# The second block's down product: tiles 0 and 1 as an eleventh pair in the second group, in place of two plain units

## The chip, the cores and the metric

The kernel runs on one core of a Trainium2 chip. The metric is the device time of one execution in microseconds (us); for each version the median of several runs is given. Engines are named as the profile names them: PE is TensorE's matmuls and PEld its weight loads, DVE is VectorE, ACT is ScalarE, POOL is GpSimd, SP is SyncE. SP and POOL do little here but issue DMA transfers; rows with SPq and POOLq are these issues.

## The reference, cut to what matters

One layer of a macaron block for 512 rows and a width of 1024, in fp32: a first feed-forward block, attention, and a second feed-forward block, which is the part that is changed. Behind it stands a last normalisation.

```python
def swiglu(x, w_gate, w_up, w_down):
    return (jax.nn.silu(x @ w_gate) * (x @ w_up)) @ w_down

x = x + 0.5 * swiglu(rmsnorm(x, ffn1_norm), ffn1_w_gate, ffn1_w_up, ffn1_w_down)
x = x + token_mixer(rmsnorm(x, mix_norm), w_in, w_out, ...)
x = x + 0.5 * swiglu(rmsnorm(x, ffn2_norm), ffn2_w_gate, ffn2_w_up, ffn2_w_down)
return rmsnorm(x, final_norm)
```

The inner width is 2816: 22 tiles of 128. Tile j of what `silu(...) * (...)` gives is called activation tile j here. In the code the first block has the name "a", the second the name "b", and buffers end in that letter.

## The kernel before

**Products in three parts.** An fp32 operand is split into a high and a low part, each of the type fp32r: ACT casts the high part, DVE subtracts it from the operand for the low one. A product is then three matmuls, high with high, high with low and low with high (`mm3`, L174 to L176), so every weight costs ACT one cast (L469) and DVE one subtraction (L473) before PE can read it.

**Seven products.** Gate, up and down are mostly computed by a scheme of Strassen's kind: a matrix product of 2 x 2 blocks by seven block products and some sums. A unit `("g", j)` or `("u", j)` gives the gate or up values of the two activation tiles j and j+1, in seven products of 12 matmuls of 256 columns; its banks are named pw, px, py, pz. The pair (j, j+1) is then kept for the down product by a chain of eleven steps (`kept`): four casts on ACT, and on DVE four low parts and three steps of sums and differences, the three largest of them of 512 columns. The results (h0, h1, h2, l0, l1, l2 and one more) go to the seven slots that `sets` names for the pair.

**The down product** adds 0.5 times `activations @ w_down` to x. It is done in two groups, `("t", 0)` for the pairs 2, 4, 6, 8, 10 and `("t", 1)` for the pairs 12, 14, 16, 18, 20. A group is seven products (a11, a22, s2, a12, s1, s3, s4 in the first, a11, s3, s2, a12, s1, a22, s4 in the second); a product takes each pair in turn, and for a pair it has two row tiles of three matmuls of 512 columns, into the banks pt. When a product ends, DVE adds its banks to x (L569), or ACT copies them into another bank. The weights are four blocks of 128x512 for each pair: a11 (buffer raa or rab, two pairs to a raw tile, of which there are three), a12 (rbb), a22 (reb) and the two sums s1 = a21 + a22 (sCb) and s3 = a11 + a21 (sBb). For a sum SP loads the first block (L523) and POOL adds the second with a transfer that accumulates (L524). s2 and s4 are made on DVE out of these blocks (L432).

**Tiles 0 and 1** of the activations do not belong to a pair in the second block. The front computes them as soon as the block begins (`gated`), splits them at once into ahb and alb (cast L927, subtraction L930), and two plain units multiply them: `("P", 0)` stands ahead of `("t", 0)` and gives the left half of the output columns, `("P", 1)` stands ahead of `("t", 1)` and gives the right half. Each has 24 matmuls of 512 columns into four banks pp, one raw tile of weights (rpb, two loads of 256 KB, split 1024 wide), and four additions to x. The first block has no plain units: there tiles 0 and 1 are multiplied in another way beside its second group.

**What sets the order.** All instructions are written out by one planner. `units` is the list of units in order; every product of one pair takes one STEP on the planner's clock (1410), and `starts` is their running sum. `at(time, rank, f)` puts an event on the planner's clock, and `run` writes them out in order of time and rank: the high part of a weight 4 STEP ahead of its product, the low part 3, a sum 5, a raw load 7, the weight sums 14. For the down groups, the table `ahead` gives for each block and pair how many STEP ahead of its group its load is issued; what isn't in it is loaded 8 STEP ahead of its product. `later` moves the split of single weights one STEP back. Each engine then runs its instructions in the order that they were written, and waits where data or a buffer isn't there. Split weights go through three places of two halves each (the buffer w in the trace), so a cast can wait for the matmuls that read what stood in that place before.

**The last product**, s4 of `("t", 1)`, is done tile by tile rather than pair by pair: its weights are all split before (`kept_weights`, kwb and kxb, at the times that TURNED_KEPT names) and its five pairs run first for one row tile and then for the other. Behind it stands the tail: squares on ACT (L2002), sums and factors on DVE (L2014 to L2016), scaling and the transfers to the output (L2025 to L2056).

## Time and profile before

| | before |
|---|---|
| runs, us | 914.67, 914.72, 916.83 (median 914.72) |
| profiled execution, us | 917.04 |
| its span, us | 915.2 |
| mean granted TensorE clock | 0.998 of full speed |
| instructions | 16047 |
| DMA | 143.88 MB, 157 GB/s mean |

The profile is of one execution; its span runs from the first to the last instruction that is recorded. A group of the profile is one line of the code, one engine and one operation, written with the buffers that it writes and reads (out<-in) and with the shape. Behind a number of instructions stand their busy time and the mean of one in ns, then the engine's idle time just before them and what ended it. A timeline row has the start in us, the duration in us, the engine and line, the operation and its buffers; in brackets stands how long the engine idled before it, and what released it. The matmuls are pipelined: the time from one start to the next is what a matmul costs, and the duration in its row is longer than that.

### The profile page before, as it was taken

What the parts mean: (1) busy time and instruction counts of PE and PEld (TensorE: products, weight loads), DVE (VectorE), ACT (ScalarE), POOL (GpSimd) and SP (SyncE); (2) the same over time, 40 slices, a digit from 0 to 9 for tenths busy, and PEclk for the clock granted to TensorE, in tenths of its full rate; (3) what the DMA queues carried; (4) which work ended last, traced back from release to release, by engine and by line L of the source; (5) the groups of instructions that cost most, each with busy time, mean ns of one, the idle gap of its engine ahead of it and who ended that gap; (6) DMA issues with size and microseconds to landing.
All of it is one profiled execution on the core that took longest, in us unless ns stands there. A gap on an engine that the chain in (4) does not pass through costs nothing.

```text
span 915.2 us, 16047 instructions
## 1 busy us (share of the span) xinstructions
PE 906.7 (99%) x5778; PEld 818.9 (89%) x5778; DVE 733.0 (80%) x1531; ACT 558.6 (61%) x1185; POOL 98.7 (11%) x123
## 2 busy tenths in 40 slices
PE   9999999999999999999999999999999999999997
PEld 7888998899998889888989778989999889999885
DVE  7698998878888886857865545898888887888886
ACT  6445765456567647656776675656666545666664
POOL 0000202121121100000000000011211212112200
PEclk9999999999999999999999999999999999999999
DMA  7354869677888613334433204365778869778822
GB/s 258 115 147 130 212 202 250 149 192 194 197 203 264 177 47 99 93 107 112 128 116 116 69 24 139 93 156 143 193 187 235 193 146 250 169 192 199 222 79 92
DMA packets 67247, 143.88 MB, mean 157 GB/s; under 512 B 7712, under 2 KB 8224, under 8 KB 67168
## 3 DMA queue, kind: packets, MB, share of 16 engines
q1 hardware_dynamic: 51312, 113.81, 38.7%
q0 software_dynamic: 15856, 29.06, 19.5%
q8 instruction: 45, 0.74, 0.3%
q14 instruction: 34, 0.28, 0.1%
HBM read 137.55 MB, written 2.14 MB: 153 GB/s over the span
## 4 chain that ended last, share of the span: by engine, by line
PE 96%; DVE 2%; ACT 1%; DMA 0%; issue 0%; DVEq 0%; SPq 0%; ACTq 0%
PE pt L176 6%; PE pt L175 6%; PE pt L174 6%; PE pq L174 2%; PE pwo L174 2%; PE pq L176 2%; PE pk L174 2%; PE pq L175 2%; PE pk L176 2%; PE pk L175 2%; PE pwo L176 2%; PE pwo L175 2%; PE pua L174 2%; PE pua L176 2%; PE pua L175 2%; PE pga L174 1%
## 5 line engine op out<-in xcount | busy, mean ns | idle before, releaser
L1736 ACT ACTIVATE pr<-pr,mx 128x128 f32<-128x128 f32 (+3 forms) x64 | 36.0, 563 | 36.7 <-DVE mx L1733 36.4
L569 DVE SCALAR_TENSOR_TENSOR x<-pt,x 128x512 f32<-128x512 f32 x52 | 34.5, 687 | 19.0 <-PE pt L176 11.7
L1733 DVE CUSTOM_DVE_ANT_0 pr<-sc,strip 128x128 f32<-128x128 f32 (+3 forms) x64 | 30.5, 489 | 23.1 <-PE sc L1731 22.6
L405 POOL DMA_DIRECT2D s1bg<-wst_dram x10 | 8.7, 866 | 331.8 <-DVE fin L1390 233.0
L473 DVE TENSOR_TENSOR w<-s2b,w 128x512 fp32r<-128x512 f32 x38 | 26.0, 685 | 7.2 <-ACT w L469 7.2
L469 ACT CAST w<-s2b 128x512 fp32r<-128x512 f32 x38 | 23.6, 620 | 7.3 <-DVE s2b L437 7.3
L469 ACT CAST w<-raa 128x512 fp32r<-128x512 f32 x31 | 18.9, 620 | 13.7 <-DVE raa L432 7.4
L174 PE MATMUL pwo<-w,mh 128*128 128x512 f32 x64 | 25.9, 405 | 0.0
L175 PE MATMUL pwo<-w,mh 128*128 128x512 f32 x64 | 25.0, 391 | 0.0
L176 PE MATMUL pwo<-w,ml 128*128 128x512 f32 x64 | 25.0, 391 | 0.0
L473 DVE TENSOR_TENSOR w<-s2a,w 128x512 fp32r<-128x512 f32 x30 | 20.6, 686 | 4.4 <-ACT w L469 4.3
L1524 DVE TENSOR_TENSOR w<-raw_qk,w 128x512 fp32r<-128x512 f32 x24 | 16.4, 687 | 7.9 <-ACT w L1520 7.8
L469 ACT CAST w<-s2a 128x512 fp32r<-128x512 f32 x30 | 18.6, 621 | 6.7 <-DVE s2a L437 6.2
L175 PE MATMUL pxgb<-ttb,w 128*128 128x256 f32 x80 | 22.5, 281 | 0.0
L469 ACT CAST w<-rab 128x512 fp32r<-128x512 f32 x26 | 15.9, 621 | 10.0 <-PE pt L176 5.6
L405 POOL DMA_DIRECT2D s1ag<-wst_dram x8 | 7.1, 887 | 130.7 <-DMA s1ag<-wst_dram 55.1
L473 DVE TENSOR_TENSOR w<-raa,w 128x512 fp32r<-128x512 f32 x31 | 20.7, 681 | 0.0
L1730 PE MATMUL sc<-k,q 128*128 128x128 f32 (+3 forms) x64 | 20.5, 322 | 0.0
L1731 PE MATMUL sc<-l,q 128*128 128x128 f32 (+3 forms) x64 | 20.2, 322 | 0.0
L175 PE MATMUL pxub<-ttb,w 128*128 128x256 f32 x72 | 20.2, 281 | 0.0
L175 PE MATMUL pwga<-xl,w 128*128 128x256 f32 x64 | 18.0, 281 | 0.0
L176 PE MATMUL pwga<-xh,w 128*128 128x256 f32 x64 | 18.0, 281 | 0.0
(1095 smaller groups left out, 3920.8 us busy)
## 6 DMA issues: line engine op xcount, KB each, us to landing
raw_qk<-wqk_dram SPq DMA_DIRECT2D x12, 512.0 KB, 3.6
raw0bg<-wst_dram SPq DMA_DIRECT2D x10, 512.0 KB, 5.5
raw0bu<-wst_dram SPq DMA_DIRECT2D x9, 512.0 KB, 5.8
raw_gua<-wgu_dram SPq DMA_DIRECT2D x8, 512.0 KB, 3.5
raw0ag<-wst_dram SPq DMA_DIRECT2D x8, 512.0 KB, 4.8
strip<-bias_rows SPq DMA_DIRECT2D x16, 256.0 KB, 4.0
raw_wo<-wo_dram SPq DMA_DIRECT2D x8, 512.0 KB, 3.4
raw0au<-wst_dram SPq DMA_DIRECT2D x7, 512.0 KB, 6.2
```

The source lines that it names most:

```text
L174: T.matmul(po, wh, mh, start=first, stop=False, skip_group_check=on)
L175: T.matmul(po, wh, ml, start=False, stop=False, skip_group_check=on)
L176: T.matmul(po, wl, mh, start=False, stop=last, skip_group_check=on)
L405: nc.gpsimd.dma_start(t[:], b, accum_op=ALU.add)
L469: A.copy(made[t][0], source(t))
L473: V.tensor_tensor(l, source(t), h.bitcast(F32), op=ALU.subtract)
L569: V.scalar_tensor_tensor(o, a, f, b, op0=ALU.mult, op1=op1)
L1524: V.tensor_tensor(l[:, c:c + 512], raw[:, c:c + 512], h[:, c:c + 512].bitcast(F32), op=ALU.subtract)
L1730: T.matmul(ps[:, :w], qs[:, qi], ks[:, :w], start=True, stop=False)
L1731: T.matmul(ps[:, :w], qs[:, qi], ls[:, :w], start=False, stop=True)
L1733: V.tensor_tensor_reduce(out=pi, in0=ps[:, :w], in1=st["b"][m][:, w - 1::-1], op0=ALU.add, op1=ALU.min, scale=1.0, scalar=3.0e38, accum_ou ...
L1736: A.activation(pi, pi, AF.Exp, scale=-1.0, bias=st["mx"][:, m, i:i + 1], accum_out=st["ls"][:, m, i:i + 1])
```

## The change

The plain units go. Tiles 0 and 1 become an ordinary pair with the number 0, the first of the second group, which then has six pairs: (0, 12, 14, 16, 18, 20). What it takes:

- The front no longer splits tiles 0 and 1. `gated` leaves them as made in the slots 0 and 1 (t1b), where ahb stood.
- `kept(0, 0, 0, 0, LATE_CHAIN)` runs the eleven steps of pair 0 at 102.5 to 121 STEP of the planner's clock, which is in the units of gate and up just behind the first group.
- Every product of the second group is one STEP longer. The four blocks s3, a12, s1 and a22 have a place for a sixth pair (slot 1, xh4, xl7), the a11 blocks fill all three raw tiles, and `later` delays the split of two a11 weights in each group by one STEP.
- The loads of s3 in the second group are issued at 70, 68, 66, 64, 6 and 20 STEP ahead of it, in place of 80, 77, 74, 71 and 11. a11, a22 and s1 have other numbers in both groups.
- `then` (12) stands where `groups[1][0]` stood, since that is now 0.

```diff
-    "b": {"plain": 2, "pairs": ((2, 4, 6, 8, 10), (12, 14, 16, 18, 20)),
-          "sets": {2: (2, 3, 24, 25, 20, 21, 26), 4: (28, 29, 30, 31, 32, 33, 34), 6: (35, 36, 37, 38, 39, 40, 41),
+    "b": {"plain": 0, "pairs": ((2, 4, 6, 8, 10), (0, 12, 14, 16, 18, 20)),
+          "sets": {0: (2, 3, 24, 25, 22, 23, 0), 2: (2, 3, 24, 25, 20, 21, 26),
+                   4: (28, 29, 30, 31, 32, 33, 34), 6: (35, 36, 37, 38, 39, 40, 41),
...
-          "s3": ((2, 28, 35, 42, 5), (20, 21, 26, 27, "xh0")),
-          "a12": (("bc", "ob", "ob", "sq", 27), (20, 21, 26, 27, "xh0")),
-          "s1": ((8, 9, 11, 10, "raw"), (10, 11, 9, 8, "xh2")),
-          "a22": (("bc", "ob", "ob", "sq", 27), ("xh3", "xl3", "xh5", "xl5", "xh7")),
-          "ahead": {"s3": ((-1.7, -2.7, -3.7, -4.7, -5.7), (80, 77, 74, 71, 11)),
-                    "s1": ((15, 17, 11, 8, 3), (15, 17, 11, 8, 9)),
-                    "a11": ((9.2, 9.1, 8.3, 8.2, 5.3), (9.2, 9.1, 8.3, 8.2, 4)),
-                    "a22": ((9, 8.5, 7, 3, 8),), "a12": ((-2.6, -3.6, -4.6, -5.6, -6.6),)}}}
+          "later": ((("t", 0), "a11", 2), (("t", 0), "a11", 3),
+                    (("t", 1), "a11", 2), (("t", 1), "a11", 3)),
+          "s3": ((2, 28, 35, 42, 5), (20, 21, 26, 27, "xh0", 1)),
+          "a12": (("bc", "ob", "ob", "sq", 27), (20, 21, 26, 27, "xh0", 1)),
+          "s1": ((8, 9, 11, 10, "raw"), (10, 11, 9, 8, "xh2", "xh4")),
+          "a22": (("bc", "ob", "ob", "sq", 27), ("xh3", "xl3", "xh5", "xl5", "xh7", "xl7")),
+          "ahead": {"s3": ((-1.7, -2.7, -3.7, -4.7, -5.7), (70, 68, 66, 64, 6, 20)),
+                    "s1": ((11.5, 14, 7.5, 4.5, 3), (12, 14, 7.5, 4.5, 5.5, 5)),
+                    "a11": ((11, 10, 5.9, 5.8, 4.6), (11, 10, 5.9, 5.8, 4.6, 4.5)),
+                    "a22": ((4.4, 4.2, 3.2, 0.5, 1.5),), "a12": ((-2.6, -3.6, -4.6, -5.6, -6.6),)}}}
...
+LATE_CHAIN = (102.5, 103.4, 103.5, 104, 105, 106, 106.5, 107.5, 109, 113, 121)
...
-TURNED_KEPT = (13, 16, 19, 22, 25)
+TURNED_KEPT = (14, 17, 20, 23, 26, 29)
...
-        units = [("g", n1)] + pairs(n1 + 2, groups[0][-1] + 2) + [("P", 0)] * (close is None) + [("t", 0)]
-        units += pairs(groups[1][0], JF) + [("P", 1)] * (close is None) + [("t", 1)]
+        units = [("g", n1)] + pairs(n1 + 2, groups[0][-1] + 2) + [("t", 0)]
+        then = groups[0][-1] + 2
+        units += pairs(then, JF) + [("t", 1)]
...
+            if final is not None:
+                kept(0, 0, 0, 0, LATE_CHAIN)
...
                 def silu():
-                    gs[j] = tp.tile([P, S], F32, tag="ptb", name=f"t1{nm}{j}")
-                    A.activation(gs[j][:], banks[j, "g"][:], AF.Silu)
+                    g.setdefault(0, {})[j] = slot(j, f"t1{nm}{j}")
+                    A.activation(g[0][j][:], banks[j, "g"][:], AF.Silu)
 
                 def up_():
-                    V.tensor_tensor(gs[j][:], banks[j, "u"][:], gs[j][:], op=ALU.mult)
-
-                def high_():
-                    ah[j] = slot(j, f"ah{nm}{j}", F32R)
-                    al[j] = slot(JF + j, f"al{nm}{j}", F32R)
-                    cast(ah[j][:], gs[j][:])
-
-                def low_():
-                    rest(al[j][:], gs[j][:], ah[j][:])
+                    V.tensor_tensor(g[0][j][:], banks[j, "u"][:], g[0][j][:], op=ALU.mult)
...
-                ev(t + 1.5, high_)
-                ev(t + 2.2, low_)
```

Lines of the changed kernel stand four or five further down than before (L473 is L478 there, L569 is L574, L753 is L758, L413 is L418, L523 is L528).

The first place is DVE at the seam ahead of the second group: the end of unit u20 and what stood in the plain unit. rab is a weight a11 of the down product, pp a bank of the plain unit, g0b, g1b and h2b belong to the chain of pair 20. Before:

```order
L569 SCALAR_TENSOR_TENSOR x_100<-pp_9569,x_100 128x512
L753 TENSOR_TENSOR h2b_9600<-g1b_9439,h1b_9566 128x512
L566 TENSOR_TENSOR g0b_9397<-g1b_9439,g0b_9397 128x256
L473 TENSOR_TENSOR w<-rab_9476,w 128x512
L569 SCALAR_TENSOR_TENSOR x_101<-pp_9570,x_101 128x512
L569 SCALAR_TENSOR_TENSOR g1b_9439<-g1b_9439,g0b_9397 128x256
L569 SCALAR_TENSOR_TENSOR g1b_9439<-g1b_9439 128x256
L473 TENSOR_TENSOR w<-rab_9497,w 128x512
L569 SCALAR_TENSOR_TENSOR x_102<-pp_9571,x_102 128x512
```

And in the change, where px and py are banks of unit u20:

```order
L478 TENSOR_TENSOR w<-rab_9339,w 128x512
L565 TENSOR_TENSOR sq<-pxub_9419,sq 128x256
L574 SCALAR_TENSOR_TENSOR g1b_9413<-sq,g1b_9413 128x512
L758 TENSOR_TENSOR h0b_9542<-g0b_9377,h0b_9542 128x256
L568 TENSOR_TENSOR g0b_9377<-pyub_9420,g0b_9377 128x256
L571 TENSOR_TENSOR g0b_9377<-g0b_9377 128x256
L478 TENSOR_TENSOR w<-rab_9453,w 128x512
L758 TENSOR_TENSOR h2b_9564<-g1b_9413,h1b_9546 128x512
L571 TENSOR_TENSOR g0b_9377<-g1b_9413,g0b_9377 128x256
```

The additions of pp have gone from between the chain and the weights, and the first weight of the group now stands among the last steps of unit u20 itself.

The second place is DVE in unit g12, the first behind the first group, where six of the eight DVE steps of pair 0's chain stand in this unit and the next. s3bu, s2b, raw0bu, raw1bu and s1bu are weights or sums of unit u12. Before:

```order
L560 TENSOR_TENSOR rbc_n_6005<-pygb_8243,rbc_n_6005 128x256
L473 TENSOR_TENSOR w<-s3bu_8155,w 128x512
L560 TENSOR_TENSOR rbc_n_6005<-pxgb_8242,rbc_n_6005 128x256
L473 TENSOR_TENSOR w<-s2b_8314,w 128x512
L473 TENSOR_TENSOR w<-raw0bu,w 128x512
L439 TENSOR_TENSOR s2b_8314<-raw0bu,s2b_8314 128x512
L473 TENSOR_TENSOR w<-s1bu_8152,w 128x512
L473 TENSOR_TENSOR w<-raw1bu,w 128x512
```

And in the change, where t1b is tile 0 or 1 as the front made it:

```order
L565 TENSOR_TENSOR rbc_n_6005<-pygb_8192,rbc_n_6005 128x256
L478 TENSOR_TENSOR w<-s3bu_8110,w 128x512
L758 TENSOR_TENSOR h0b_8282<-t1b_6437,h0b_8282 128x256
L571 TENSOR_TENSOR t1b_6437<-t1b_6437 128x256
L565 TENSOR_TENSOR rbc_n_6005<-pxgb_8191,rbc_n_6005 128x256
L478 TENSOR_TENSOR w<-s2b_8263,w 128x512
L758 TENSOR_TENSOR h2b_8323<-t1b_6517,h1b_8302 128x512
L478 TENSOR_TENSOR w<-raw0bu,w 128x512
L571 TENSOR_TENSOR t1b_6437<-t1b_6517,t1b_6437 128x256
L444 TENSOR_TENSOR s2b_8263<-raw0bu,s2b_8263 128x512
L478 TENSOR_TENSOR w<-s1bu_8107,w 128x512
L478 TENSOR_TENSOR w<-raw1bu,w 128x512
```

The steps of pair 0 have come between the weights; the weights' own order is as it was.

The third place is SP's queue around unit g12, where the s3 blocks of the second group (sBb) are issued among the raw tiles of gate and up (raw0bg, raw1bg, raw0bu, raw1bu) and the weight sums (s1bg, s3bg). Before:

```order
L413 DMA raw0bg<-wst_dram 128x1024
L523 DMA sBb_8169<-wdg_dram 128x512
L413 DMA raw1bg<-wst_dram 128x512
L523 DMA sBb_8203<-wdg_dram 128x512
L523 DMA sBb_8232<-wdg_dram 128x512
L413 DMA raw0bu<-wst_dram 128x1024
L404 DMA s1bg_8274<-wst_dram 128x512
L404 DMA s3bg_8277<-wst_dram 128x512
L413 DMA raw1bu<-wst_dram 128x512
L523 DMA sBb_8296<-wdg_dram 128x512
```

And in the change:

```order
L418 DMA raw0bg<-wst_dram 128x1024
L418 DMA raw1bg<-wst_dram 128x512
L418 DMA raw0bu<-wst_dram 128x1024
L528 DMA sBb_8185<-wdg_dram 128x512
L409 DMA s1bg_8223<-wst_dram 128x512
L409 DMA s3bg_8226<-wst_dram 128x512
L418 DMA raw1bu<-wst_dram 128x512
L528 DMA sBb_8231<-wdg_dram 128x512
L528 DMA sBb_8265<-wdg_dram 128x512
L528 DMA sBb_8306<-wdg_dram 128x512
```

The first three sBb blocks have moved behind loads of gate and up, and the four follow each other at the distance of two STEP.

More of the change, by code (lines that the diff above doesn't have):

```diff
@@ L389, in sum_slots @@
                 return LAST_SUMS[u[0] == "u"]
-            if u[1] == groups[1][0]:
+            if u[1] == then:
                 return GROUP_SUMS[u[0] == "u"]
@@ L842, in pipeline @@
                             seen[s0] = u
-                            if u[0] == "g" and u[1] in groups[1][:2] and final is None:
+                            if u[0] == "g" and u[1] in (then, then + 2) and final is None:
                                 time += STEP
-                            if u == ("g", groups[1][0]) and final is not None:
+                            if u == ("g", then) and final is not None:
                                 time += 3 * STEP
                             at(time, 1, weight_sums, u)
-                        if final is None and u != ("g", groups[1][0]):
+                        if final is None and u != ("g", then):
                             at(starts[t] - 7 * STEP, 1.5, load, u)
@@ L930, in rest @@
                 V.tensor_tensor(o, a, h.bitcast(F32), op=ALU.subtract)
-            first_w, banks, ts, gs = {}, {}, {}, {}
+            first_w, banks, ts = {}, {}, {}
             nx.extend(slot(i, f"nx{nm}{k}") for k, i in enumerate(TURNED_NORMED))
```

## The prediction

> **What bounds the kernel now.** I read the page's busy times first, then the chain of waits, then tables by stage, then the timeline around the places that the change touches.
>
> ```profile
> PE 906.7 (99%) x5778; PEld 818.9 (89%) x5778; DVE 733.0 (80%) x1531; ACT 558.6 (61%) x1185; POOL 98.7 (11%) x123
> ...
> PE 96%; DVE 2%; ACT 1%; DMA 0%; issue 0%; DVEq 0%; SPq 0%; ACTq 0%
> ```
>
> TensorE (PE) is busy for 99% of the span and 96% of the chain that ended last runs through it. So time comes off only where matmuls go away, or where PE waits. The second view is the table of stages. Its columns after the stretch are its length, then busy time of PE, weight loads, VectorE (DVE), ScalarE (ACT) and POOL, then the granted clock and the share and rate of the DMA engines.
>
> ```profile
> 762.00:772.00 10.00, 10.00 (x87) 10.00 (x86) 5.95 (x11) 5.97 (x13) 2.62 (x3) 1.00 1.02 265
> 772.00:782.00 10.00, 10.00 (x87) 10.00 (x86) 9.62 (x20) 6.88 (x15) 1.78 (x2) 1.00 0.76 170
> 852.00:862.00 10.00, 10.00 (x61) 8.86 (x60) 9.02 (x18) 5.37 (x11) 3.33 (x5) 1.00 1.04 245
> 862.00:872.00 10.00, 10.00 (x46) 8.29 (x45) 9.43 (x16) 6.94 (x12) 0.00 (x0) 1.00 0.51 170
> ```
>
> PE is full at full clock in all four, and DVE is close behind it in three. DVE makes the low half of every weight that PE reads, so it is the engine that could become the bound. Only 762 to 772 has real room on it (5.95 of 10).
>
> **The matmuls.** The plain units run from the first pp row to the first pt row behind it, twice.
>
> ```profile
> 703.06 0.40 PE L174 MATMUL pp<-w,ahb 128*128 128x512 f32 x1
> ...
> 708.51 0.39 PE L174 MATMUL pt<-w,h0b 128*128 128x512 f32 x1
> ...
> 855.51 0.40 PE L174 MATMUL pp<-w,ahb 128*128 128x512 f32 x1
> ...
> 861.00 0.39 PE L174 MATMUL pt<-w,h0b 128*128 128x512 f32 x1
> ...
> 865.08 0.39 PE L174 MATMUL pt<-w,h0b 128*128 128x512 f32 x1
> ```
>
> They take 708.51 - 703.06 = 5.45 and 861.00 - 855.51 = 5.49, together 10.94 us for 48 matmuls. A pair as seven products costs 7 x 2 x 3 = 42 matmuls of the same shape. From 861.00 to 865.08 stand 18 of them (three pairs of one product), 4.08 / 18 = 0.227 us each. So 42 x 0.227 = 9.52 us. The first few behind a switch of shape run a little slower (the 24 above took 0.05 more than 24 x 0.227), and that stays. I take **6 x 0.227 = 1.36 us off**, bounds 1.3 and 1.42.
>
> [...]
>
> **The front.** Tiles 0 and 1 are no longer split at once, so two casts leave ACT and two subtractions DVE near 598 and 611 us.
>
> ```profile
> 611.69 0.69 DVE L930 TENSOR_TENSOR alb<-t1b,ahb 128x512 fp32r<-128x512 f32 x1
> ...
> 612.90 0.69 DVE L473 TENSOR_TENSOR w<-raw0bg,w 128x512 fp32r<-128x512 f32 x1
> ...
> 613.39 0.28 PE L175 MATMUL pwgb<-xl,w 128*128 128x256 f32 x1
> 613.64 0.39 PE L176 MATMUL pwgb<-xh,w 128*128 128x256 f32 x1
> 613.87 0.28 PE L174 MATMUL pwgb<-xh,w 128*128 128x256 f32 x1
> ```
>
> Steps on PE here are 0.12 us; 613.39 to 613.64 and on to 613.87 are 0.25 and 0.23. The low half that begins at 612.90 ends at 613.59, and 613.64 is the matmul that reads it. With the row at 611.69 gone it ends up to 0.6 earlier. That is worth between 0 and 0.24 us; I take **0.2**, since both delayed matmuls sit right at that wait.
>
> **The eleven steps on pair 0, in the next units.** Five are 256 wide and three are 512 wide on DVE, four are casts on ACT.
>
> ```profile
> L753 DVE TENSOR_TENSOR h2b<-g1b,h1b 128x512 fp32r<-128x512 f32 x5 | 3.4, 683 | 0.0
> ...
> L753 DVE TENSOR_TENSOR h0b<-g0b,h0b 128x256 fp32r<-128x256 f32 x5 | 2.1, 417 | 0.0
> ...
> 768.60 0.69 DVE L473 TENSOR_TENSOR w<-raw1bu,w 128x512 fp32r<-128x512 f32 x1 [0.73 <-ACT w L469]
> 770.02 0.69 DVE L473 TENSOR_TENSOR w<-s2b,w 128x512 fp32r<-128x512 f32 x1 [0.73 <-ACT w L469]
> 771.93 0.42 DVE L563 TENSOR_TENSOR g0b<-pwub,g0b 128x256 f32<-128x256 f32 x1 [1.22 <-PE pwub L176]
> ...
> 779.71 0.68 DVE L473 TENSOR_TENSOR w<-s1bg,w 128x512 fp32r<-128x512 f32 x1
> ...
> 781.91 0.28 PE L176 MATMUL pygb<-txb,w 128*128 128x256 f32 x1
> ```
>
> That is 3 x 0.683 + 5 x 0.417 = 4.1 us of DVE. The order puts six of the eight (2.8 us) between the rows that here lie at 763 to 770 us, where DVE idles 0.73 + 0.73 + 1.22 us and more before; these are covered. The other two, 0.6 us of issue each, fall one into the stretch 772 to 782, which is full, and one behind it. There the tightest weight is s1bg: low half done at 779.71 + 0.68 = 780.39, read at 781.91, 1.5 us to spare. One op takes 0.6 of it, 0.9 is left. So **0**; without that cover the 4.1 us would come through less 1.5, at most 2.6 us. ACT's four casts (about 0.5 us of issue each) lie in the same stretches, in which it is 60 to 69% busy. What is queued behind them on both engines is the weights just named.
>
> **The two seams.** The plain units stood between the last pair of gate and up and the down products, and gave DVE and ACT 5.45 us to finish that pair's split and the first weights. The first block has no such units at its own seam:
>
> ```profile
> 281.94 0.28 PE L176 MATMUL pyua<-xh,w 128*128 128x256 f32 x1
> 282.06 0.40 PE L174 MATMUL pt<-w,h0a 128*128 128x512 f32 x1
> ...
> 283.06 0.69 DVE L473 TENSOR_TENSOR w<-raa,w 128x512 fp32r<-128x512 f32 x1
> ...
> 284.83 0.39 PE L174 MATMUL pt<-w,h0a 128*128 128x512 f32 x1
> ```
>
> PE goes from unit to product in 0.12 us. The twelve matmuls from 282.06 to 284.83 take 2.77 us, 0.05 over 12 x 0.227, and the third weight is done at 283.75, 1.5 us before its matmul at 285.3 (284.83 plus two steps). The changed order on DVE is this one, name for name. In the second block the plain units also brought work of their own, which goes too:
>
> ```profile
> L569 DVE SCALAR_TENSOR_TENSOR x<-pp,x x8: 678/680/685, 704.7 to 861.9; 128x512 f32<-128x512 f32 x8
> ...
> L473 DVE TENSOR_TENSOR w<-rpb,w x2: 1215/1215/1215, 700.8 to 853.2; 128x1024 fp32r<-128x1024 f32 x2
> ...
> 862.47 1.28 DVE L473 TENSOR_TENSOR w<-rab,w 128x512 fp32r<-128x512 f32 x2
> ```
>
> Per seam that is 4 x 0.68 + 1.2 = 3.9 of the 5.5 us, so DVE loses 1.6 net. The tightest weight behind the seam is the first of the two at 862.47: done 863.15, read two steps after 865.08, at 865.53, so 2.4 us to spare and 0.8 after the loss. **0** again. If the 3.9 were not given back, 2.4 - 5.5 = -3.1 us a seam.
>
> On the queues, POOL has two more adding loads and SP two more rows. Three s3 blocks are now issued behind the loads of one more unit, near 760 us, and are read near 864, so they have some 100 us. What counts on SP at the seam are the raw tiles:
>
> ```profile
> 847.58 1.54 SPq L510 DMA_DIRECT2D rab<-wdg_dram  x2
> ...
> 854.46 0.33 SPq L510 DMA_DIRECT2D rab<-wdg_dram  x1
> ...
> DMA to landing us min/median/max: 3.9/5.4/6.5
> ```
>
> The row at 854.46 had to wait for the plain weights' tile; without them the third tile follows the second, near 850, and lands by 856.5 (the longest of these rows, 6.5). Its first matmul comes at 855.51 + 4 x 1.36 = 861.0; a cast and a subtraction take 1.3, so 3 us are left.
>
> **The second group.** Each of its seven products is one pair longer: 1.36 us of PE each, 9.5 in all, against nine DVE ops (seven low halves, two sums) of 0.68, 6.2 us. The additions to x stay as many. DVE gets easier there, and the loads (seven of 256 KB in place of four) go where the DMA share is 0.51.
>
> **The end.**
>
> ```profile
> 894.09 0.39 PE L176 MATMUL pt<-w,h4b 128*128 128x512 f32 x1
> ...
> 894.52 0.69 DVE L569 SCALAR_TENSOR_TENSOR x<-pt,x 128x512 f32<-128x512 f32 x1 [0.49 <-PE pt L176]
> ...
> 908.33 0.72 ACT L2037 ACTIVATE x<-x,fin 128x512 f32<-128x512 f32 x1 [0.68 <-DVE fin L2016]
> ...
> 908.37 0.39 PE L176 MATMUL pt<-kxb,h2b 128*128 128x512 f32 x1
> ...
> 908.95 0.58 ACT L2002 ACTIVATE junk<-pt 128x512 f32<-128x512 f32 x1
> ```
>
> A bank is read 0.43 us after its last matmul starts (894.09 to 894.52). The last square starts 0.58 after its own, because ACT is still on the tile before. In the change the last product has 18 matmuls for each tile and not 15, so tile 2 is through 3 x 0.227 = 0.68 earlier against the end, and the square starts by the matmul: 0.15 us. From there to the end, 915.2 - 908.95 = 6.25 us, nothing changes. Bounds 0 and 1.36 (all that the a22 chain gains in time); I take **0.15**, for the square reads the bank of that very matmul.
>
> **Sum.** 1.36 + 0.2 + 0.15 = 1.7 us off the profiled span of 915.2, which gives 913.5. That execution itself took 917.04, 1.84 around its span, and is above the three runs (median 914.72, highest 916.83); I take the same 1.7 off the median: **913.0 us**, own range 912.5 to 913.8.
>
> **Rivals.**
> - *The end was not waiting for matmuls but for its own chain.* Then the whole 1.36 us that the longer last product gives the a22 chain comes off the end instead of 0.15: 913.0 - 1.2, about 911.8, and with the front and matmul terms at their upper ends 911.6. For it: ACT and DVE hand over to each other all through the last 12 us. Against: the last square follows its matmul within 0.58 us, and only 0.15 of that isn't the handover.
> - *A seam without its cover (slower).* If DVE or ACT can't use the time given back, because ACT's casts wait for a weight place and the split of pair 10 or 20 sits behind them, the wait decides from a loss of 2.4 us on, and costs up to 3.1 a seam: 913.0 + 3.1 = 916.1 with one, 919.2 with both. Against: the first block's seam, in the same order.
> - *Pair 0's steps make DVE late in the gate unit of pair 14.* It decides from 1.5 us at s1bg; up to 2.6 us: 913 to 915.6. Against: the idle rows quoted.
> - *The change doesn't do what it says.* The order shows 6 matmul rows fewer, and nothing plain; I give it nothing.
>
> **How the numbers follow.** Forecast 0.68, end chain 0.14, seams 0.10 (0.09 of it over the bound below), pair 0 0.08. A measurement of this kernel can tell about 0.3% from no change, 2.74 us: faster means below 911.98, slower above 917.46. The forecast, the pair 0 case and the mildest seam are within it (0.77). The end-chain case is just past it on the fast side (0.14), two seams on the slow side (0.09). The range runs from 911.7, which takes in most of the end-chain case, to 915.6, the top of the pair 0 case.
>
> **What would show it.** Right: no pp rows, PE's last matmul about 1.6 us earlier at 906.8, steps of 0.12 across both seams, 613.39 to 613.64 closed to 0.12, the last square 0.43 behind its matmul. Wrong: a step over 0.3 us on PE near 697 to 705, 770 to 780 or 850 to 858 with DVE w or a DMA as its releaser, or a tail longer than 6.3 us behind the last square.

## The result and the profile after

| | before | changed |
|---|---|---|
| runs shown with the change: median, us | 915.08 (22 runs) | 913.53 (22 runs) |
| lowest and highest, us | 914.42, 917.44 | 912.88, 915.92 |
| span of the profiled execution, us | 915.2 | 911.4 |

The ratio is 0.9985 with a 95% interval of 0.9978 to 0.9992, which is 0.7 to 2.0 us of 915. The medians lie 1.55 us apart. The forecast was 913.0 us, 1.7 less than the 914.72 us of the first three runs; over 22 runs the kernel before has a median of 915.08, so 0.36 of the 0.53 us between forecast and result are in the base. The change makes the kernel faster by an amount that is real and smaller than the 3.02 us (0.33%) over which the 22 runs of the kernel before lie.

The first lines of the changed kernel's page, busy times and the chain that ended last:

```profile
PE 903.7 (99%) x5772; PEld 816.6 (90%) x5772; DVE 733.4 (80%) x1536; ACT 561.3 (62%) x1192; POOL 100.4 (11%) x125
...
PE 98%; DVE 1%; ACT 0%; DMA 0%; issue 0%; DVEq 0%; SPq 0%; ACTq 0%
```

PE has 3.0 us less to do and is as full as before. The two spans differ by 3.8 us (915.19 and 911.35), more than twice what the medians do, so the first question is where that is. I laid the starts of PE's matmuls in the two traces beside each other. Here is the first stretch of PE before:

```profile
5.64 0.79 PE L1194 MATMUL pga<-eha,w 128*128 128x512 f32 x1 [0.86 <-ACT w L1174]
6.23 0.63 PE L1194 MATMUL pua<-eha,w 128*128 128x512 f32 x1
...
9.64 0.39 PE L1194 MATMUL pua<-eha,w 128*128 128x512 f32 x1
```

And the same ten matmuls in the changed kernel (lines behind those that went stand three further up there):

```profile
5.00 0.50 PE L1191 MATMUL pga<-eha,w 128*128 128x512 f32 x1 [0.23 <-ACT w L1171]
5.34 0.40 PE L1191 MATMUL pua<-eha,w 128*128 128x512 f32 x1
...
7.17 0.39 PE L1191 MATMUL pua<-eha,w 128*128 128x512 f32 x1
```

From 6.23 to 9.64 stand eight steps of 0.43 us, in the other trace eight of 0.23: in the profiled execution of the kernel before, PE took about 0.43 us a matmul for 4 us (5.64 to 9.64). It also began 0.64 us later (5.64 and 5.00). Nothing of this belongs to the change, and it is 2.47 of the 3.8 us: 0.64 for the start and 1.83 for the longer steps, and this 1.83 is most of the 3.0 us that PE is busy less. The places behind it, in the changed kernel's timeline of PE (front, both seams, end):

```profile
611.12 0.28 PE L179 MATMUL pwgb<-xl,w 128*128 128x256 f32 x1
611.24 0.28 PE L180 MATMUL pwgb<-xh,w 128*128 128x256 f32 x1
611.36 0.28 PE L178 MATMUL pwgb<-xh,w 128*128 128x256 f32 x1
...
700.44 0.27 PE L180 MATMUL pyub<-xh7m,w 128*128 128x256 f32 x1
700.55 0.40 PE L178 MATMUL pt<-w,h0b 128*128 128x512 f32 x1
...
847.63 0.28 PE L180 MATMUL pyub<-xh7m,w 128*128 128x256 f32 x1
847.75 0.40 PE L178 MATMUL pt<-w,h0b 128*128 128x512 f32 x1
...
904.68 0.39 PE L180 MATMUL pt<-kxb,h2b 128*128 128x512 f32 x1
...
905.17 0.60 ACT L1999 ACTIVATE junk<-pt 128x512 f32<-128x512 f32 x1 [1.56 <-PE pt L180]
```

The two steps of 0.25 and 0.22 us of the front are gone (0.12 each), and PE passes from the last unit into each down group in 0.11 and 0.12 us. The last square now starts 0.49 us behind its matmul, and ACT waits for PE ahead of it. With the rows of the kernel before, the sum reads:

| place | rows before | rows after | us |
|---|---|---|---|
| start of the kernel, and its steps of 0.43 | to 9.64 | to 7.17 | -2.47 |
| attention, near 355 us | two steps of 0.12 | 0.22 each | +0.20 |
| front of the second block | steps of 0.25 and 0.22 | 0.12 twice | -0.24 |
| first plain unit | 703.06 to 708.51 | gone | -5.45 |
| unit g14, a new wait | 784.40 to 784.64 | 776.45 to 776.87 | +0.18 |
| second plain unit | 855.51 to 861.00 | gone | -5.49 |
| second group, 42 matmuls more | 861.00 to 908.37 | 847.75 to 904.68 | +9.56 |
| behind the last matmul | 6.82 | 6.67 | -0.15 |

The first two lines come and go between executions. The other six are the change: -0.24 - 5.45 + 0.18 - 5.49 + 9.56 - 0.15 = -1.59 us. The 1.55 us between the medians agree with it; their interval is too wide to confirm any of the small terms, which rest on the traces.

The table of stages around the pair's chain and the second seam, changed kernel, same columns as in the prediction:

```profile
754.00:764.00 10.00, 10.00 (x87) 10.00 (x86) 7.69 (x17) 6.37 (x15) 4.35 (x5) 1.00 1.05 269
764.00:774.00 10.00, 10.00 (x87) 10.00 (x86) 9.71 (x20) 7.25 (x15) 1.75 (x2) 1.00 0.97 240
844.00:854.00 10.00, 10.00 (x62) 8.91 (x61) 8.10 (x18) 6.13 (x12) 4.35 (x6) 1.00 1.00 236
854.00:864.00 10.00, 10.00 (x46) 8.29 (x45) 10.00 (x17) 7.18 (x13) 0.00 (x0) 1.00 0.90 259
```

Seven of the eight DVE steps of pair 0 stand in the first two stretches: DVE has 7.69 in place of 5.95 there and 9.71 in place of 9.62. The one in the second stretch (at 770.23) makes DVE late, and PE waits 6 us later. DVE and PE there, changed kernel:

```profile
770.23 0.68 DVE L758 TENSOR_TENSOR h4b<-t1b,h3b 128x512 fp32r<-128x512 f32 x1
...
775.58 0.68 DVE L478 TENSOR_TENSOR w<-raw0bu,w 128x512 fp32r<-128x512 f32 x1
776.18 0.42 DVE L565 TENSOR_TENSOR rbc_n<-pygb,rbc_n 128x256 f32<-128x256 f32 x1
...
776.45 0.28 PE L180 MATMUL pxgb<-ttb,w 128*128 128x256 f32 x1
776.65 0.39 PE L178 MATMUL pygb<-xh1m,w 128*128 128x256 f32 x1
776.87 0.28 PE L179 MATMUL pygb<-xl1m,w 128*128 128x256 f32 x1
```

And the same rows in the kernel before:

```profile
783.52 0.41 DVE L560 TENSOR_TENSOR rbc_n<-pygb,rbc_n 128x256 f32<-128x256 f32 x1
...
784.40 0.28 PE L176 MATMUL pxgb<-ttb,w 128*128 128x256 f32 x1
784.51 0.28 PE L174 MATMUL pygb<-xh1m,w 128*128 128x256 f32 x1
784.64 0.28 PE L175 MATMUL pygb<-xl1m,w 128*128 128x256 f32 x1
```

The last product of a gate unit adds to the bank pygb, which DVE must have read before. In the changed kernel DVE's read ends at 776.18 + 0.42 = 776.60, and the matmul starts at 776.65. In the other gate units of this block, before and after, the read mostly ends 0.57 us ahead of that matmul (0.38 at least), and the matmul follows the one ahead of it by 0.12.

### The profile page after: what moved, and what is told of

Same layout as the page of the kernel before. It is cut to its first block, busy times and chain, and to the rows that moved or that the text cites. A ratio compares the mean times of both kernels' runs of the same rounds, so it can differ in the third digit from the quotient of the medians.

```text
span 911.4 us, 16044 instructions
## 1 busy us (share of the span) xinstructions
PE 903.7 (99%) x5772; PEld 816.6 (90%) x5772; DVE 733.4 (80%) x1536; ACT 561.3 (62%) x1192; POOL 100.4 (11%) x125
## 4 chain that ended last, share of the span: by engine, by line
PE 98%; DVE 1%; ACT 0%; DMA 0%; issue 0%; DVEq 0%; SPq 0%; ACTq 0%
PE pt L178 7%; PE pt L180 7%; PE pt L179 7%; PE pq L178 2%; PE pwo L178 2%; PE pq L179 2%; PE pq L180 2%; PE pk L178 2%; PE pk L180 2%; PE pk L179 2%; PE pwo L179 2%; PE pwo L180 2%; PE pua L178 2%; PE pua L180 2%; PE pua L179 2%; PE pga L178 1%
## 5 line engine op out<-in xcount | busy, mean ns | idle before, releaser
L574 DVE SCALAR_TENSOR_TENSOR x<-pt,x 128x512 f32<-128x512 f32 x52 | 34.5, 688 | 19.1 <-PE pt L180 11.6
L478 DVE TENSOR_TENSOR w<-s2b,w 128x512 fp32r<-128x512 f32 x38 | 26.1, 686 | 8.0 <-ACT w L474 8.0
L179 PE MATMUL pwo<-w,mh 128*128 128x512 f32 x64 | 25.0, 391 | 0.0
L478 DVE TENSOR_TENSOR w<-s2a,w 128x512 fp32r<-128x512 f32 x30 | 20.6, 686 | 4.4 <-ACT w L474 4.3
L179 PE MATMUL pxgb<-ttb,w 128*128 128x256 f32 x80 | 22.5, 281 | 0.0
L478 DVE TENSOR_TENSOR w<-raa,w 128x512 fp32r<-128x512 f32 x31 | 20.7, 682 | 0.0
L179 PE MATMUL pxub<-ttb,w 128*128 128x256 f32 x72 | 20.2, 281 | 0.0
L478 DVE TENSOR_TENSOR w<-rab,w 128x512 fp32r<-128x512 f32 x28 | 18.8, 686 | 0.0
L179 PE MATMUL pwga<-xl,w 128*128 128x256 f32 x64 | 18.0, 281 | 0.0
```

The lines of the kernel that those rows point to most:

```text
L179: T.matmul(po, wh, ml, start=False, stop=False, skip_group_check=on)
L478: V.tensor_tensor(l, source(t), h.bitcast(F32), op=ALU.subtract)
L574: V.scalar_tensor_tensor(o, a, f, b, op0=ALU.mult, op1=op1)
```

## The experiments

**The front's split put back.** In the changed kernel, both tiles are split in the front again, into two free slots that nothing reads.

```diff
+                def high_():
+                    ah[j] = slot(JF, f"ah{nm}{j}", F32R)
+                    al[j] = slot(JF + 1, f"al{nm}{j}", F32R)
+                    cast(ah[j][:], g[0][j][:])
+
+                def low_():
+                    rest(al[j][:], g[0][j][:], ah[j][:])
...
+                ev(t + 1.5, high_)
+                ev(t + 2.2, low_)
```

> The changed kernel with the four steps of the front put back: tiles 0 and 1 are split as before (two casts on ACT, two subtractions on DVE), into two free slots that nothing reads. The output stays the reference's. My theory (the split of tile 1 made DVE late for the first product of unit g2): the two steps of 0.25 us in that product come back, and from there on PE is 0.25 us (0.2 to 0.3) later than in the changed kernel, all other distances the same. Rival (the two steps had another cause, such as the new loads): the product stays even at 0.12 us a matmul and nothing moves.

The time was 915.60 us, one run. PE and DVE in the front of this kernel:

```profile
609.67 0.69 DVE L937 TENSOR_TENSOR alb<-t1b,ahb 128x512 fp32r<-128x512 f32 x1
...
611.37 0.28 PE L179 MATMUL pwgb<-xl,w 128*128 128x256 f32 x1
611.63 0.39 PE L180 MATMUL pwgb<-xh,w 128*128 128x256 f32 x1
611.85 0.28 PE L178 MATMUL pwgb<-xh,w 128*128 128x256 f32 x1
```

The steps of 0.26 and 0.22 are back, and PE falls 0.24 us behind the changed kernel there. So the split in the front is the cause. But this run lost 1.64 us more at a place that it does not touch, and 0.26 us behind it in unit g14. DVE and PE in unit u12, and the landing times of the ten raw0bg tiles:

```profile
766.93 0.69 DVE L442 TENSOR_TENSOR s2b<-s1bg,raw0bg 128x512 f32<-128x512 f32 x1 [2.04 <-DMA raw0bg<-wst_dram]
...
766.99 0.28 PE L180 MATMUL pxub<-ttb,w 128*128 128x256 f32 x1
768.65 0.39 PE L178 MATMUL pyub<-xh1m,w 128*128 128x256 f32 x1 [1.39 <-DVE sq L565]
...
DMA to landing us min/median/max: 3.5/5.6/12.0
```

The raw tile of unit g14 landed 12.0 us after its issue. DVE waited 2.0 us for it, and behind DVE's wait stood its read of the bank pyub, on which PE waits, as in g14 above. I come back to this two experiments on.

**Where the steps of pair 0 lie.** Two versions of the table of the chain, one with a second large step in the full stretch, one with the large step that stands there (at 770.23) moved to a place where DVE idles:

```diff
-LATE_CHAIN = (102.5, 103.4, 103.5, 104, 105, 106, 106.5, 107.5, 109, 113, 121)
+LATE_CHAIN = (102.5, 103.4, 103.5, 104, 105, 106, 106.5, 107.5, 109, 113, 113.2)
...
+LATE_CHAIN = (102.5, 103.4, 103.5, 104, 105, 106, 106.5, 107.5, 109, 108.5, 121)
```

> The changed kernel with the last step of pair 0's chain (128x512 on DVE, l1) at 113.2 STEP in place of 121, which puts a second large step into the full stretch of unit g14. Theory A, from the trace of the changed kernel (PE's product s4 of g14 accumulates into bank py, which DVE must have read first; DVE's read was 0.6 us late there and ended 0.05 before the matmul): one more step of 0.6 us makes the same wait 0.6 us longer, 0.8 in all in place of 0.2, and everything behind it 0.6 later. Theory B, as my prediction had it (what DVE is late for is the weight s1bg, with 1.5 us to spare): two steps are 1.2 us, still under 1.5, and the wait stays at 0.2 or less.

The time was 914.51 us, one run. PE and DVE in unit g14, with the second step:

```profile
774.39 0.28 PE L180 MATMUL pwgb<-xh7m,w 128*128 128x256 f32 x1
774.89 0.38 PE L178 MATMUL pygb<-txb,w 128*128 128x256 f32 x1 [0.22 <-ACT pygb L562]
...
777.56 0.42 DVE L565 TENSOR_TENSOR rbc_n<-pygb,rbc_n 128x256 f32<-128x256 f32 x1
...
777.72 0.28 PE L180 MATMUL pxgb<-ttb,w 128*128 128x256 f32 x1
778.03 0.39 PE L178 MATMUL pygb<-xh1m,w 128*128 128x256 f32 x1
```

This execution was 0.78 us later than the changed kernel's before this place, so DVE's read would have begun at 776.18 + 0.78 = 776.96; it began at 777.56, 0.60 later, and the matmul again followed its end (777.98) by 0.05. PE is 0.60 later behind this place, as theory A has it. The loss stands in two pieces only because an ACT copy, held up by another late raw tile, stopped PE behind 774.39 for 0.49 us and so took most of the same wait ahead of it. What carries theory A here is DVE's read, 0.60 us later with no idle time of DVE ahead of it, and the matmul right behind its end. Theory B falls.

> The changed kernel with the step l0 of pair 0's chain (128x512 on DVE) at 108.5 STEP in place of 113, into a place of unit u12 where DVE idles for 1.0 us ahead of its multiplication by bank pw. Theory A: the wait of 0.2 us in g14's product s4 goes, DVE's read of py ends 0.57 us ahead of the matmul as in the other gate units, and PE is 0.2 us earlier from there on. Theory B (the wait has another cause, for instance the weights): it stays at 0.2 us. A multiplication that comes late in u12 would show as a new wait on PE at g14's first products.

The time was 914.35 us, one run. The wait in g14 went, but the raw tile of g14 landed after 10.8 us in this run, DVE waited 0.65 us for it in u12, and PE lost 0.26 us behind that. PE lost another 0.38 us in the second group, at the first weight of s2 (868.99 to 869.47 in place of a step of 0.23). The last two a11 tiles had landed 9.2 and 9.9 us after their issue (7.6 and 8.6 in the changed kernel); ACT waited 2.25 us for one, and from there to the weight of s2 DVE was 1.3 us later against PE than in the changed kernel. The run does not decide between the gain and the loss; the version was tried again with the cause of the late tile taken away.

**The s3 loads that stand ahead of the raw tile.** In the changed kernel SP issues three s3 loads in a row and then raw0bg of g14. DVE first reads that tile 10.4 us after its issue (753.98 to 764.33 in the trace of the changed kernel; 11.6 in that of before, 760.69 to 772.28). Three versions, all run on one chip: the changed kernel again, the loads spread over four units, and the spread together with the early step.

```diff
-          "ahead": {"s3": ((-1.7, -2.7, -3.7, -4.7, -5.7), (70, 68, 66, 64, 6, 20)),
+          "ahead": {"s3": ((-1.7, -2.7, -3.7, -4.7, -5.7), (66, 59, 52, 45, 6, 20)),
```

> The changed kernel once more, as it is, beside the next two on the same chip. It gives a second trace of the same instructions. My theory from the runs so far (the raw tile raw0bg of unit g14 is issued right behind three loads of s3 blocks, lands 10 to 12 us later, and DVE needs it 10.4 us after its issue): that landing is again 10 to 12 us, and where it is over 10.4 the product s4 of u12 waits on PE for as much less 0.5 us. Median 913.2 to 913.9. Rival (the late landings came from the steps added in those runs): 9 us or less and no wait.

> The changed kernel with the first four s3 loads of the second group at 66, 59, 52 and 45 STEP ahead in place of 70, 68, 66 and 64, that is one in each unit from g12 on in place of three in a row ahead of raw0bg of g14. Theory (three loads in a row, with their adding loads, hold up raw0bg): raw0bg of g14 lands within 8.8 us of its issue, as at most in the kernel before, DVE never waits for it, the wait in u12 never appears, and the median is 0.1 to 0.5 us under that of the changed kernel, with fewer runs over 915. The 0.2 us wait in g14's s4 stays. Rival (the landing is late because the raw tile itself comes behind the weight sums of two units): still 10 us or more, and the median is that of the changed kernel within 0.1 us.

> The same spread of the s3 loads, and besides the step l0 of pair 0's chain at 108.5 STEP in place of 113, in the place of u12 where DVE idles. Theory: both waits that the change brought into the units u12 and g14 are gone; PE runs from 620 us to its last matmul without a step over 0.06 us beyond the usual ones; 0.2 us less than with the spread alone, median about 912.9 to 913.3. Rival (the chain's step makes DVE late at u12 instead): a wait of 0.1 to 0.3 us at u12's product s4, and the same median as with the spread alone.

| | median of 11 runs, us | ratio to the kernel before and 95% interval |
|---|---|---|
| changed kernel again | 913.65 | 0.9984 (0.9975 to 0.9993) |
| s3 spread | 913.52 | 0.9986 (0.9977 to 0.9995) |
| s3 spread, early step | 913.55 | 0.9985 (0.9976 to 0.9995) |

The landing times of raw0bg (least, median, most), first of the changed kernel, then with the spread:

```profile
DMA to landing us min/median/max: 3.4/5.4/10.2
...
DMA to landing us min/median/max: 3.9/5.6/6.7
```

The longest landing falls from 10.2 to 6.7 us, and to 6.8 in the two other traces with the spread. In the ten traces with the three loads in a row (the changed kernel twice and eight experiments) it was 7.4 to 12.0, and in three of them DVE waited for it. So the row of loads is shown as the cause, together with the transfers that POOL adds to them; which of the two holds the tile up is open. The gain that I expected in the median is not shown: in seven of the ten traces the tile came in time, and the medians are the same within 0.13 us. I had expected fewer runs over 915 us, too; of 11 each it was none for the changed kernel, one with the spread and three with the early step besides. Of the changed kernel's second run I expected a landing of 10 us or more; it took 9.8 and nothing waited.

With the spread the early step can be read alone. PE in unit g14, spread and early step:

```profile
778.40 0.28 PE L180 MATMUL pxgb<-ttb,w 128*128 128x256 f32 x1
778.52 0.28 PE L178 MATMUL pygb<-xh1m,w 128*128 128x256 f32 x1
778.64 0.28 PE L179 MATMUL pygb<-xl1m,w 128*128 128x256 f32 x1
```

The wait is gone, no new one appeared in u12, and PE gains 0.2 us there (its lag against the changed kernel goes from 1.96 to 1.77 us). I had expected it in the median too, but 0.2 us can't be seen in a median of 11 runs.

**The seams.** The third a11 weight of each down group has its low half computed 3 and 5 times over, which delays everything behind it on DVE.

```diff
-            V.tensor_tensor(l, source(t), h.bitcast(F32), op=ALU.subtract)
+            again = 4 if final is not None and ops[t][0][0] == "t" and ops[t][1][0] == "a11" and ops[t][2] == 2 else 0
+            for _ in range(1 + again):
+                V.tensor_tensor(l, source(t), h.bitcast(F32), op=ALU.subtract)
```

> The changed kernel with the low half of the third a11 weight of each down group computed three times over in place of once: 2 more DVE operations of 128x512 (0.6 us of issue each) at each seam, where DVE has no idle time. Theory (the seams are covered; in the trace of the changed kernel the tightest weight behind either seam, the fourth a11, is done 1.30 us before its third matmul): 2 x 0.6 = 1.2 us fits, and PE shows no step over 0.1 us beyond the usual at 700 to 712 and 848 to 860 us. Rival (a seam without its plain unit has no cover): 1.2 us more on PE at each seam.

> The same with 4 more operations at each seam. Theory: 4 x 0.6 = 2.4 us, 1.1 over what is to spare, so PE waits 1.1 us (0.8 to 1.4) behind each seam, about 2.2 in all, at the fourth a11 weight. Rival (no cover): 2.4 at each. Rival (DVE has idle time there that the trace does not show as such): nothing.

The times were 914.01 and 917.43 us, one run each. In the traces PE lost 0.54 and 0.50 us at the two seams with two added operations, and 2.02 and 2.01 with four. PE at the second seam, with four:

```profile
852.78 0.39 PE L178 MATMUL pt<-w,h0b 128*128 128x512 f32 x1
854.69 0.50 PE L179 MATMUL pt<-w,h0b 128*128 128x512 f32 x1 [1.52 <-DVE w L480]
```

Both numbers are above what I expected (0 and 1.1) and under those of no cover. Two of my figures were off. A repeated operation took 0.73 us and not 0.6, so the doses were 1.46 and 2.9 us. And the low half is read by the second of a pair's matmuls (L179, the row above), not by the third, so the third weight's spare time in the changed kernel is 703.50 - 702.23 = 1.27 us and the fourth's 1.1. Then 1.46 - 1.27 and 2.9 - 1.27 give 0.2 and 1.6 us; the rest, 0.3 to 0.4, goes at the restarts (the matmul that waited takes 0.1 us longer to the next) and at the fourth weight, where a second, short stop follows. So the seams have 1.1 to 1.3 us to spare and no more.

**The old numbers of the loads.** In the changed kernel, the loads of a11, a22 and s1 got the numbers of the kernel before, and the two delayed splits were taken out.

```diff
-          "later": ((("t", 0), "a11", 2), (("t", 0), "a11", 3),
-                    (("t", 1), "a11", 2), (("t", 1), "a11", 3)),
...
-                    "s1": ((11.5, 14, 7.5, 4.5, 3), (12, 14, 7.5, 4.5, 5.5, 5)),
-                    "a11": ((11, 10, 5.9, 5.8, 4.6), (11, 10, 5.9, 5.8, 4.6, 4.5)),
-                    "a22": ((4.4, 4.2, 3.2, 0.5, 1.5),), "a12": ((-2.6, -3.6, -4.6, -5.6, -6.6),)}}}
+                    "s1": ((15, 17, 11, 8, 3), (15, 17, 11, 8, 9, 8)),
+                    "a11": ((9.2, 9.1, 8.3, 8.2, 5.3), (9.2, 9.1, 8.3, 8.2, 4.6, 4.5)),
+                    "a22": ((9, 8.5, 7, 3, 8),), "a12": ((-2.6, -3.6, -4.6, -5.6, -6.6),)}}}
```

> The changed kernel with the numbers of the kernel before for the loads of a11, a22 and s1 of the second block (a11 9.2, 9.1, 8.3, 8.2 and so on, a22 at 9, 8.5, 7, 3, 8), and without the delay of two a11 splits. The output stays the reference's. Theory (the seam is covered by how DVE and ACT stand in it; the tables matter little): at the first seam the third and fourth a11 land about 1 us later, their casts stand in front of pair 10's split on ACT, and PE waits 0 to 0.8 us; nothing at the second. Rival (the tables are what covers the seams): up to 3.1 us at the first and as much at the second.

It took 929.97 us, one run, and it failed as an experiment. The numbers count back from the start of a group, and without the plain unit that start is 3.9 STEP (5440 / 1410) nearer to unit g10. So the a22 load into rbc_n, at 9 STEP, falls into that unit while it still keeps its own sum there: the load is issued at 695.14, DVE waits 5.7 us for it and then adds a bank to what it has brought. The second block computes with an overwritten buffer, against what the expectation says of the output. SP shows the other half, one row of its queue in this kernel:

```profile
679.58 6.23 SPq L526 DMA_DIRECT2D sCb<-wdg_dram  x2
```

Two s1 loads held SP for 6.2 us until their slots came free, with the raw tiles of unit u10 queued behind them. Behind PE's waits of 2.87 us (to 692.60) and 3.65 us (to 702.29) the matmuls of 256 columns also came every 0.21 us in place of 0.12, from 693.9 to 697.1 and from 702.7 to 707.4; the mean granted clock of this run was 0.993, against 0.999 in the changed kernel. The run says that the new numbers were needed because the seam moved; it says nothing of what the seam itself costs.

**The end.** Pairs of the last product are left out, one (6 matmuls) and three (18).

```diff
                         for q in range(n):
+                            if 1 <= q <= 3:
+                                continue
```

> The changed kernel without pair 12 in its last product (s4 of the second group): 6 matmuls of 512 columns are left out, 3 for each row tile, so that part of the output lacks that pair's share. Theory A (the end follows PE's last matmul): PE's last matmul comes 6 x 0.227 = 1.36 us earlier, and the span ends 6.83 us behind its start as in the kernel before (6.72 in the changed one), so 1.25 us are gained. Rival (the end waits for its own chain on ACT and DVE): the last matmul comes 1.36 us earlier and the end moves by less than 0.4 us.

> The changed kernel without pairs 12, 14 and 16 in its last product: 18 matmuls of 512 columns are left out, so that part of the output lacks the share of these pairs. Theory (the end follows PE's last matmul until the two row tiles of the last product are closer than the 2.5 us that one tile's chain holds ACT): the last matmul comes 18 x 0.227 = 4.08 us earlier; the tiles are then 2.04 us apart, so the last square starts about 1.0 us behind its matmul in place of 0.49, and the span ends about 7.2 us behind the last matmul's start in place of 6.72: 3.6 us gained. Rival (the chain of the end is the bound): less than 1.5 us gained.

The times were 912.09 and 912.07 us, one run each, with spans of 910.33 and 910.30. PE was 0.37 and 0.77 us later than in the changed kernel before it came to the end, so the ends moved by 1.4 and 1.8 us. With six left out the last matmul starts at 903.65 and ACT waits 0.35 us for it; the gain is the whole of the 1.4 us, and the rival falls for that size. With 18 left out, ACT at the end:

```profile
900.48 1.34 ACT L2025 ACTIVATE x<-x,fin 128x512 f32<-128x512 f32 x2 [0.82 <-DVE fin L2015]
901.73 0.58 ACT L2001 ACTIVATE junk<-pt 128x512 f32<-128x512 f32 x1
...
903.50 0.72 ACT L2036 ACTIVATE x<-x,fin 128x512 f32<-128x512 f32 x1 [0.68 <-DVE fin L2015]
904.13 0.58 ACT L2001 ACTIVATE junk<-pt 128x512 f32<-128x512 f32 x1
```

The last matmul starts at 901.38 and its square 2.75 us later: ACT goes from one tile to the next without waiting for PE. Of 4.1 us of matmuls only 1.8 came through, half of what I expected. I had reckoned with one tile's chain, 0.5 us; what holds ACT is the chain of the two tiles ahead as well (the scaling at 900.48). So the end does have a bound of its own, and in the changed kernel it lies 1.8 us under PE's.

**All the findings in one.** The spread and the early step, and one warm-up matmul more at the start of the kernel.

```diff
-WARM = 8
+WARM = 9
```

> The version with the spread s3 loads and the early step, with 9 warm-up matmuls ahead of the kernel in place of 8, which fills the idle time of PE ahead of its first real matmul (0.2 to 0.9 us in the traces so far). [...]

The median of 11 runs was 913.40 us, from 912.61 to 913.79, with a ratio of 0.9978 (0.9969 to 0.9987). No run is over 915. I had expected that, and a median of 912.7 to 913.4. Of the 55 runs of the changed kernel and its two variants with eight warm-up matmuls 9 were, so 11 without one would come about by chance once in seven times ((46/55)^11 = 0.14): that the ninth warm-up matmul keeps late starts like that of the kernel before away was my estimate, and the runs don't settle it (the last section has what the traces say of the start). In the trace PE had no idle time ahead of its first real matmul at 5.00 us, and steps of 0.23 from 5.90 on. This is the fastest version of all, 0.13 us in the median under the changed kernel, which is within what the intervals leave open.

## Why the prediction held

*Six matmuls less.* 1.36 us was forecast; the rows give 5.45 + 5.49 - 9.56 = 1.38. Shown by the trace, and the step of 0.227 us by all rows.

*The front.* 0.2 was forecast within 0 to 0.24; 0.24 came, and putting the split back took 0.24 again. That it came out so close has some luck in it: DVE reached the weight not 0.6 us earlier, as forecast, but 2.3 (608.28 in place of 612.90, less the 2.28 us that the whole execution was ahead there), because the split of tile 0 had held it up as well. PE had only 0.24 to win.

*The end.* 0.15 was forecast, and the span's end came 0.15 nearer to the last matmul. Only 0.09 of this is what the forecast meant (the last square at 0.49 us behind its matmul in place of 0.58, and not at 0.43); the rest lies behind the square, where I had expected nothing to change. The rival that the end was bound by its own chain had 0.14. It was wrong at this size, though the bound that it spoke of exists 1.8 us further down, for ACT's work on the two tiles ahead and not only on the last.

*Pair 0's chain costs nothing.* This step was wrong by 0.2 us. I looked for the weight that DVE would bring late (s1bg, 1.5 us to spare) and left out the other thing that PE waits for from DVE, its reading of a bank that the next product adds to. There only 0.57 us were to spare, less than the 0.60 of one 128x512 operation. The place was right, the unit g14, and the price is far below the 2.6 us at which I bounded it, because all of the eight steps but one were covered.

*The seams cost nothing.* Right: 0.11 and 0.12 us from the last matmul of the unit to the first of the group. I had 0.8 us left at the tightest weight; the trace has 1.1, and the runs with added operations show that PE waits for what goes beyond 1.1 to 1.3. The forecast's figure was one step of 0.23 too large, since it took the third matmul of a pair, and not the second, as the reader of the low half. It also had DVE easier in the second group. The stretch from 854 to 864 above shows the contrary: DVE is busy for all of its 10.00 us, where it had 9.43 in the kernel before. PE lost nothing to that in the changed kernel, but the run with the early step alone lost 0.38 us there.

*The queues.* I held the three s3 loads for harmless because their own data are needed 100 us later. What I did not ask is what stands behind them in SP's queue: a raw tile that is needed 10.4 us later. That is a loss of 0 in seven of the ten traces and of up to 1.64 us on PE in the others (the run with the front's split), which no term of the sum had. The third a11 tile of the second group was forecast to land 6.5 us after its issue at most, with 3 us left; its two halves took 7.6 and 8.6.

So the three terms of the sum were 1.38 + 0.24 + 0.15 = 1.77 us where 1.7 was forecast, and the wait in g14 took 0.18 of them: 1.59. Without the starts of the two executions, PE's last matmul came 1.4 us earlier, where 1.6 was forecast.

## What to carry to other kernels

A product that adds to a bank can wait for the engine that reads the bank, not only for its weights (here at 776.65 us, 0.05 behind the end of DVE's read): list both when asking how late an engine may be, and take the smaller. When loads are moved to a quieter time, look at what is queued behind them and how soon that is needed, not at when their own data are (here a raw tile that is needed 10.4 us after its issue landed after 7.4 to 12.0 us behind three loads in a row, and after 6.7 to 6.8 with them spread). When a span is compared with another, line up the starts of one engine's instructions over the whole program first: here nearly two thirds of the difference lay 600 us ahead of the change.

## What the runs showed of the hardware

PE's first real matmuls, of 512 columns, stood 0.43 us apart in some executions before the step became 0.23, and when it did differs between executions of nearly the same instructions: in 11 of the 13 traces with eight warm-up matmuls the steps of 0.23 begin at 5.2 to 7.2 us, in two (the kernel before, and the spread with the early step) at 9.64 and 9.36 us. The spread with and without the early step both have their first real matmul at 5.43 us; the tenth stands at 9.36 us with it and at 7.63 us without. That is 1.73 us, more than the whole change.

The two late ones had PE idle for 0.86 and 0.66 us between the warm-up matmuls and the first real one. The trace of the spread alone had 0.65 us there, and its steps were 0.34 us and then 0.24 from 5.77 us on, so the pause alone does not decide it; the other ten had 0 to 0.50 us. What sets the time of the change was not shown.

The column of the granted clock is 1.00 for 0 to 9.6 us of the kernel before all the same, because its record only begins at 9.62, so in a table of stages the steps of 0.43 us have to be read from the starts of the matmuls.

A DVE operation of 128x512 that is repeated on the same operands came every 0.73 us (with four added operations the five begin at 701.59 and the operation behind them at 705.09), where different ones of that size come every 0.60 (770.23 to 770.83 in the changed kernel); and the matmul that had waited took 0.34 us to the next one (705.23 to 705.57 with four added) where others take 0.227.
